# Contrast adjustment on one core: 64 KB rows in three buffers, tiles moved in four transfers of every 4th row, the arithmetic shared by ScalarE and VectorE

## The chip, the cores and the metric

One Trainium2 chip, one of its cores. The metric is the device time of one execution in microseconds (us), median of several runs. The profile's span is about 2 us shorter than the timed run (before: 237.3 against 239.31). Engines: DVE is VectorE, ACT is ScalarE, PE is TensorE, SP issues the loads. "DMA engines" are the core's 16 transfer engines.

## The reference

```python
x: float32 [16, 3, 512, 512]; factor = 1.5
mean = np.mean(x, axis=(2, 3), keepdims=True)
return np.clip(mean + factor * (x - mean), 0, 1).astype(np.float32)
```

Each image plane (1 MB) needs its mean before any of its pixels can be written. 50.33 MB come in and 50.33 MB go out.

## The kernel before

Twelve tiles of 128 rows by 8192 columns (4.2 MB) in a ring of six buffers. DVE and ACT sum each row in two parts; two small matmuls with a block matrix add the rows of an image and give the shift; DVE scales and clips in place.

```python
ROW = 8192; BUFS = 6; SHORT = 2048; SUM = 4352
...
def compute(t):
    xt = ring[:, t % BUFS, :]
    nc.vector.tensor_reduce(out=own[:, 0:1], in_=xt[:, 0:SUM], ...)
    nc.scalar.activation(out=junk, in_=xt[:, SUM:ROW], func=Act.Copy, accum_out=own[:, 1:2])
    # two matmuls: shift = bias[:, t : t + 1] (PSUM)
    for n in FIRST if t == 0 else [ROW]:
        nc.vector.tensor_scalar(out=part, in0=part, scalar1=factor, scalar2=shift, op0=mult, op1=add)
        nc.vector.tensor_scalar(out=part, in0=part, scalar1=0.0, scalar2=1.0, op0=max, op1=min)
        store(t, c, c + n)          # issued by ACT, 128 rows
...
load(0, c1=SHORT); load(0, c0=SHORT); load(1); load(2, n=2); load(4, n=2)   # issued by SP
for t in range(n_tiles):
    compute(t)
    if t + BUFS < n_tiles:
        load(t + BUFS)              # waits until the store of tile t has landed
```

## Time and profile before

| | before |
|---|---|
| time, median of 5 runs beside the changed kernel | 239.30 us |
| span of the profile | 237.3 us |
| DVE / ACT busy | 163.1 / 43.2 us |
| bytes moved, mean rate | 100.66 MB, 424 GB/s |

The DMA row has "9" in all slices but the first and last, and the span is the bytes over the mean rate, 100.66 MB at 424 GB/s = 237.4 us.

### The profile page before, as it was taken

The page shows a single profiled execution, that of the slowest core. Times are in us where ns is not written, and L with a number is a line of the kernel's source. Part 1 is how long each engine was busy: PE and PEld are TensorE (multiplying, and loading weights), DVE is VectorE, ACT ScalarE, POOL GpSimd, SP SyncE. Part 2 cuts the span into 40 slices and gives each one's busy share as a digit, 9 for nine tenths or more (in the row PEclk, how much of TensorE's full clock was granted, in tenths as well). Part 3 has the DMA queues.
Part 4 walks back from the last instruction along what each step waited for, and adds up shares of the span by engine and source line. Part 5 has one row for each costly group of instructions (what it writes and reads, how often), then busy time and mean ns, then how long its engine had stood idle before and what let it go on. Part 6 is the DMA issues. An engine that isn't in the chain of part 4 may idle for free.

```text
span 237.3 us, 285 instructions
## 1 busy us (share of the span) xinstructions
PE 14.1 (6%) x48; PEld 12.0 (5%) x48; DVE 163.1 (69%) x38; ACT 43.2 (18%) x25; POOL 0.9 (0%) x9
## 2 busy tenths in 40 slices
PE   0010010001010001010010100100100100010000
PEld 0010010001010001010010100100100100010000
DVE  0079989048989328999989898891892795687000
ACT  2050230041050023050320504101400500500000
POOL 1000000000000000000000000000000000000000
DMA  7999999999999999999999999999999999999996
GB/s 297 410 442 442 421 442 359 456 439 441 442 436 414 403 431 442 442 442 442 436 442 436 414 409 425 442 442 442 442 436 442 436 420 403 425 442 442 442 442 265
DMA packets 3712, 100.66 MB, mean 424 GB/s; under 512 B 384, under 2 KB 384, under 8 KB 384
## 3 DMA queue, kind: packets, MB, share of 16 engines
q1 hardware_dynamic: 1840, 50.33, 49.7%
q10 hardware_dynamic: 1872, 50.33, 49.2%
HBM read 50.33 MB, written 50.33 MB: 424 GB/s over the span
## 4 chain that ended last, share of the span: by engine, by line
DMA 57%; DVE 29%; another core or an unknown queue 3%; PE 1%; SPq 1%; issue 0%; DVEq 0%
DMA ring<-in_x_dram 41%; DMA out_dram<-ring 16%; DVE sums L81 10%; DVE ring L91 9%; DVE ring L94 9%; PE bias L87 1%; SPq L76 1%; DVEq L91 0%
## 5 line engine op out<-in xcount | busy, mean ns | idle before, releaser
L81 DVE TENSOR_REDUCE sums<-ring 128x1 f32<-128x4352 f32 x12 | 56.2, 4683 | 45.7 <-DMA ring<-in_x_dram 45.7
L84 ACT ACTIVATE junk<-ring 128x3840 f32<-128x3840 f32 x12 | 40.8, 3403 | 163.3 <-DMA ring<-in_x_dram 107.5
L91 DVE TENSOR_SCALAR ring<-ring,bias 128x8192 f32<-128x8192 f32 (+2 forms) x13 | 54.1, 4163 | 8.9 <-PE bias L87 7.4
L94 DVE TENSOR_SCALAR ring<-ring 128x8192 f32<-128x8192 f32 (+2 forms) x13 | 53.3, 4099 | 0.4
L86 PE MATMUL bias<-sums,blockw 128*128 128x1 f32 x24 | 7.0, 361 | 190.8 <-ACT junk L84 190.8
L86 PEld LDWEIGHTS bias<-sums,blockw 128*128 128x128 f32 x24 | 6.0, 312 | 191.7 <-ACT junk L84 175.2
L87 PE MATMUL bias<-sums,blockw 128*128 128x1 f32 x24 | 7.0, 363 | 4.3 <-DVE sums L81 3.9
L87 PEld LDWEIGHTS bias<-sums,blockw 128*128 128x128 f32 x24 | 6.0, 311 | 5.3 <-DVE sums L81 5.0
L84 ACT ACTIVATION_READ_ACCUMULATOR junk<-ring 128x1 f32 x12 | 2.2, 186 | 0.0
L84 ACT ACT_TABLE_LOAD x1 | 1.3, 1283 | 0.7 <-PEq L129 0.7
L63 POOL MEMSET blockw<- 32x32 f32 x4 | 0.5, 117 | 0.2
L61 POOL MEMSET blockw<- 128x128 f32 x1 | 0.2, 204 | 0.3 <-POOLq L129 0.3
L129 POOL MEMSET const-bfloat16-1.0<- 128x1 bf16 x1 | 0.1, 111 | 0.0
L129 POOL MEMSET const-uint8-127<- 128x1 uint8 x1 | 0.1, 111 | 0.0
L129 POOL MEMSET const-float32-1.0<- 128x1 f32 x1 | 0.1, 108 | 0.0
L129 POOL MEMSET const-float32-0.0<- 128x1 f32 x1 | 0.1, 103 | 0.2 <-issue 0.2
## 6 DMA issues: line engine op xcount, KB each, us to landing
out_dram<-ring ACTq DMA_DIRECT2D x11, 4096.0 KB, 35.8
ring<-in_x_dram SPq DMA_DIRECT2D x7, 4096.0 KB, 49.7
ring<-in_x_dram SPq DMA_DIRECT2D x2, 8192.0 KB, 66.7
ring<-in_x_dram SPq DMA_DIRECT2D x1, 3072.0 KB, 11.7
out_dram<-ring ACTq DMA_DIRECT2D x1, 3072.0 KB, 28.2
ring<-in_x_dram SPq DMA_DIRECT2D x1, 1024.0 KB, 4.8
out_dram<-ring ACTq DMA_DIRECT2D x1, 1024.0 KB, 17.5
```

The source lines that it names most:

```text
L61: nc.gpsimd.memset(blockw, 0.0)
L63: nc.gpsimd.memset(blockw[a : a + ppi, a : a + ppi], wconst)
L76: nc.sync.dma_start(out=ring[:, b : b + n, c0:c1], in_=src)
L81: nc.vector.tensor_reduce(out=own[:, 0:1], in_=xt[:, 0:SUM], axis=mybir.AxisListType.X, op=Alu.add)
L84: nc.scalar.activation(out=junk, in_=xt[:, SUM:ROW], func=Act.Copy, accum_out=own[:, 1:2])
L86: nc.tensor.matmul(shift, blockw, own[:, 1:2], start=True, stop=False)
L87: nc.tensor.matmul(shift, blockw, own[:, 0:1], start=False, stop=True)
L91: nc.vector.tensor_scalar(out=part, in0=part, scalar1=factor, scalar2=shift, op0=Alu.mult, op1=Alu.add)
L94: nc.vector.tensor_scalar(out=part, in0=part, scalar1=0.0, scalar2=1.0, op0=Alu.max, op1=Alu.min)
L129: nc = _bacc.Bacc("TRN2", target_bir_lowering=False, num_devices=1)
```

## The change

Its intent: fewer and larger packets (64 KB rows); buffers given back in quarters, so that three double-size buffers do as well as six; a lighter DVE. A quarter is every 4th row of the tile, 32 rows.

```diff
-ROW = 8192
-BUFS = 6
+ROW = 16384
+BUFS = 3
+OWN = 5120
+CHUNKS = (6144, 5120)
+PARTS = 4
...
+        ext = bass.AP(tensor=..., offset=(t * P + q) * ROW + c0,
+            ap=[[parts * ROW, P // parts], [1, c1 - c0]])
+        rows = ring[q::parts, t % BUFS, c0:c1]
...
+        nc.scalar.activation(out=xt[:, SUM:ROW], in_=xt[:, SUM:ROW], func=Act.Copy, accum_out=...)
...                                                  # DVE does its own columns 0:OWN, then
+        for n in CHUNKS:
+            nc.scalar.activation(out=part, in_=part, func=Act.Relu, bias=shift, scale=factor)
+            nc.vector.tensor_scalar(out=part, in0=part, scalar1=1.0, scalar2=None, op0=Alu.min)
...
+            if t == 0: store(t, parts=PARTS, c1=SHORT)      # an early store of 256 KB
...
         load(0, c1=SHORT)
         load(0, c0=SHORT)
         load(1)
-        load(2, n=2)
-        load(4, n=2)
+        load(2)
         for t in range(n_tiles):
             compute(t)
+            if t == n_tiles - 1:                            # last tile: two column pieces, 128 rows each
+                store(t, c1=cut); store(t, c0=cut)
+            elif t + BUFS < n_tiles:
+                for q in range(PARTS): store(t, q, PARTS, ...)
+                for q in range(PARTS): load(t + BUFS, q, PARTS)
+            else:
+                store(t)
```

So the first three loads and the last three stores are whole (128 rows), and the stores of tiles 0 to 2 and the loads of tiles 3 to 5 are quarters (32 rows).

More of the change, by code (lines that the diff above doesn't have):

```diff
@@ L10 @@
 P = 128
-ROW = 8192
-BUFS = 6
+ROW = 16384
+BUFS = 3
 SHORT = 2048
-FIRST = (SHORT, ROW - SHORT)
-SUM = 4352
+OWN = 5120
+CHUNKS = (6144, 5120)
+SUM = 8704
+PARTS = 4
 @with_exitstack
@@ L39 @@
     assert ppi * ROW == n_pix and per_tile * n_tiles == n_img
+    assert OWN + sum(CHUNKS) == ROW
     factor = float(factor)
@@ L45 @@
     out_f = out.rearrange("b c h w -> (b c h w)")
-    def dram(ap, t, c0=0, c1=ROW):
-        return bass.AP(tensor=ap.tensor, offset=t * P * ROW + c0, ap=[[ROW, P], [1, c1 - c0]])
-    consts = ctx.enter_context(tc.tile_pool(name="consts", bufs=1))
     xpool = ctx.enter_context(tc.tile_pool(name="xpool", bufs=1))
@@ L53 @@
     psum = ctx.enter_context(tc.tile_pool(name="psum", bufs=1, space=bass.MemoryType.PSUM))
-    sums = small.tile([P, 2 * n_tiles], f32, name="sums")
-    junk = small.tile([P, ROW - SUM], f32, name="junk")
-    bias = psum.tile([P, n_tiles], f32, name="bias")
-    blockw = consts.tile([P, P], f32, name="blockw")
-    nc.gpsimd.memset(blockw, 0.0)
-    for a in range(0, P, ppi):
-        nc.gpsimd.memset(blockw[a : a + ppi, a : a + ppi], wconst)
-    ring = xpool.tile([P, BUFS, ROW], f32, name="ring")
@@ L68, in load @@
-    def load(t, c0=0, c1=ROW, n=1):
-        b = t % BUFS
-        src = bass.AP(
-            tensor=x_f.tensor,
-            offset=t * P * ROW + c0,
-            ap=[[ROW, P], [P * ROW, n], [1, c1 - c0]],
-        )
-        nc.sync.dma_start(out=ring[:, b : b + n, c0:c1], in_=src)
+    ring = xpool.tile([P, BUFS, ROW], f32, name="ring")
+    sums = small.tile([P, n_tiles, 2], f32, name="sums")
+    bias = small.tile([P, n_tiles], f32, name="bias")
+    pbias = psum.tile([P, n_tiles], f32, name="pbias")
@@ new lines, with move @@
+    blockw = small.tile([P, P], f32, name="blockw")
+    nc.gpsimd.memset(blockw, 0.0)
+    for a in range(0, P, 2 * ppi):
+        mid, end = a + ppi, a + 2 * ppi
+        nc.gpsimd.memset(blockw[a:end, mid:end], wconst)
+        nc.gpsimd.memset(blockw[a:mid, mid:end], 0.0)
+        nc.gpsimd.memset(blockw[a:mid, a:mid], wconst)
+    def move(engine, to, source, t, q, parts, c0, c1):
+        ext = bass.AP(
+            tensor=(source if to is ring else to).tensor,
+            offset=(t * P + q) * ROW + c0,
+            ap=[[parts * ROW, P // parts], [1, c1 - c0]],
+        )
+        rows = ring[q::parts, t % BUFS, c0:c1]
+        if to is ring:
+            engine.dma_start(out=rows, in_=ext)
+        else:
+            engine.dma_start(out=ext, in_=rows)
@@ L78, in compute, with load, store @@
+    def load(t, q=0, parts=1, c0=0, c1=ROW):
+        move(nc.sync, ring, x_f, t, q, parts, c0, c1)
+    def store(t, q=0, parts=1, c0=0, c1=ROW):
+        move(nc.scalar, out_f, ring, t, q, parts, c0, c1)
     def compute(t):
         xt = ring[:, t % BUFS, :]
-        own = sums[:, 2 * t : 2 * t + 2]
         nc.vector.tensor_reduce(
-            out=own[:, 0:1], in_=xt[:, 0:SUM], axis=mybir.AxisListType.X, op=Alu.add
+            out=sums[:, t, 0:1], in_=xt[:, 0:SUM], axis=mybir.AxisListType.X, op=Alu.add
@@ L83, in compute @@
         )
-        nc.scalar.activation(out=junk, in_=xt[:, SUM:ROW], func=Act.Copy, accum_out=own[:, 1:2])
-        shift = bias[:, t : t + 1]
-        nc.tensor.matmul(shift, blockw, own[:, 1:2], start=True, stop=False)
-        nc.tensor.matmul(shift, blockw, own[:, 0:1], start=False, stop=True)
-        c = 0
-        for n in FIRST if t == 0 else [ROW]:
-            part = xt[:, c : c + n]
-            nc.vector.tensor_scalar(
-                out=part, in0=part, scalar1=factor, scalar2=shift, op0=Alu.mult, op1=Alu.add
-            )
-            nc.vector.tensor_scalar(
-                out=part, in0=part, scalar1=0.0, scalar2=1.0, op0=Alu.max, op1=Alu.min
-            )
-            store(t, c, c + n)
+        nc.scalar.activation(
+            out=xt[:, SUM:ROW],
+            in_=xt[:, SUM:ROW],
+            func=Act.Copy,
+            accum_out=sums[:, t, 1:2],
+        )
@@ new lines, in compute @@
+        for j in (1, 0):
+            nc.tensor.matmul(
+                pbias[:, t : t + 1], blockw, sums[:, t, j : j + 1], start=j == 1, stop=j == 0
+            )
+        shift = bias[:, t : t + 1]
+        nc.vector.tensor_copy(out=shift, in_=pbias[:, t : t + 1])
+        own = xt[:, 0:OWN]
+        nc.vector.tensor_scalar(
+            out=own, in0=own, scalar1=factor, scalar2=shift, op0=Alu.mult, op1=Alu.add
+        )
+        nc.vector.tensor_scalar(
+            out=own, in0=own, scalar1=0.0, scalar2=1.0, op0=Alu.max, op1=Alu.min
+        )
@@ L98, in compute @@
+        c = OWN
+        for n in CHUNKS:
+            part = xt[:, c : c + n]
+            nc.scalar.activation(out=part, in_=part, func=Act.Relu, bias=shift, scale=factor)
+            nc.vector.tensor_scalar(out=part, in0=part, scalar1=1.0, scalar2=None, op0=Alu.min)
             c += n
-    def store(t, c0, c1):
-        nc.scalar.dma_start(out=dram(out_f, t, c0, c1), in_=ring[:, t % BUFS, c0:c1])
+            if c == ROW:
+                break
+            if t == 0:
+                store(t, parts=PARTS, c1=SHORT)
@@ L106 @@
         load(1)
-        load(2, n=2)
-        load(4, n=2)
+        load(2)
         for t in range(n_tiles):
             compute(t)
-            if t + BUFS < n_tiles:
-                load(t + BUFS)
+            if t == n_tiles - 1:
+                cut = ROW - CHUNKS[-1]
+                store(t, c1=cut)
+                store(t, c0=cut)
+            elif t + BUFS < n_tiles:
+                for q in range(PARTS):
+                    store(t, q, PARTS, c0=SHORT if t + q == 0 else 0)
+                for q in range(PARTS):
+                    load(t + BUFS, q, PARTS)
+            else:
+                store(t)
 _INS = ['x', 'factor']
```

## The prediction

> **What bounds the kernel now.** I read the page's engine table and its 40 slices first. In the slices below, the first line is DVE's busy tenths, the second the DMA engines', the third the GB/s they moved; the two queue lines give packets, bytes and the share of all 16 engines' span.
>
> ```profile
> span 237.3 us, 285 instructions
> ...
> DVE  0079989048989328999989898891892795687000
> ...
> DMA  7999999999999999999999999999999999999996
> GB/s 297 410 442 442 421 442 359 456 439 441 442 436 414 403 431 442 442 442 442 436 442 436 414 409 425 442 442 442 442 436 442 436 420 403 425 442 442 442 442 265
> ...
> q1 hardware_dynamic: 1840, 50.33, 49.7%
> q10 hardware_dynamic: 1872, 50.33, 49.2%
> ```
>
> The DMA engines are at "9" in every slice but the first and last, and the two queues (q1 loads, q10 stores) fill 98.9% of the span between them. DVE (69%) has empty slices, ACT (18%) hardly works. The kernel is one uninterrupted transfer of 100.66 MB.
>
> Next the table by stages (stretch in us, its length, each engine's busy time, clock, DMA share, GB/s): loads and stores mixed, then the end, when only stores are left.
>
> ```profile
> 21.00:60.00 39.00, 2.35 (x8) 2.00 (x8) 28.66 (x7) 6.99 (x4) 0.00 (x0) 1.00 0.99 417
> 60.00:203.70 143.70, 9.39 (x32) 8.02 (x32) 113.49 (x26) 27.97 (x16) 0.00 (x0) 1.00 1.01 434
> 203.70:236.00 32.30, 1.18 (x4) 1.01 (x4) 13.60 (x3) 3.50 (x2) 0.00 (x0) 1.00 0.98 422
> ```
>
> The rate is the same whoever computes, so computing hides beside the transfers. That holds in the tail too: the last tile comes in at 203.8 and its store is issued at 218.2 us, while the store queue is still draining.
>
> ```profile
> 203.76 4.69 DVE L81 TENSOR_REDUCE sums<-ring 128x1 f32<-128x4352 f32 x1 [4.98 <-DMA ring<-in_x_dram]
> ...
> 218.17 0.34 ACTq L101 DMA_DIRECT2D out_dram<-ring  x1
> ```
>
> Last the waits of the load queue (waits in total us, times, longest): loads wait 139 us for stores to free a buffer, and it costs nothing, because the engines then work on those very stores.
>
> ```profile
> SPq L76 <- DMA out_dram<-ring: 138.9, 7, 25.5
> ```
>
> The chain of waits gives DVE 29%, but I don't take that as a bound: it steps through tiles whose computing ran under full DMA engines.
>
> **The floor in packets.** The trace's DMA packet records give the usual duration of one row's packet: 309 ns for 8 KB, 912 for 24 KB, 1213 for 32 KB. The last step is 301 ns per 8 KB (27.2 GB/s an engine) and about 8 ns are left over as fixed cost. One engine carries 8 rows of each 128-row transfer: per direction 8 x 309 + 8 x 912 + 88 x 1213 = 116.5 us, 233.0 for both. (Check: 116.5 / 237.3 = 49.1%, and the page has 49.2% for q10.) The first packet starts at 1.7 us, the last ends at 236.0: 234.3 us, thus 1.3 us idle in all. About 1.3 us follow.
>
> [...]
>
> **The change, part by part.**
> *Rows of 64 KB.* Half as many packets. A 64 KB packet should take 8 x 301 + 8 = 2417 ns, against 2 x 1213 = 2426. In the new count (8 x 309 + 8 x 2118 + 40 x 2417 = 116.1 us per direction, the stores the same within 0.1) this makes 232.2 us against 233.0: **0.8 us gained**, on the path.
> *Computing per tile (8.4 MB, 6 of them).* DVE: reduce of 8704, at most 2 x 4683 = 9.3 us; copy of the shift 0.2 (my guess); from the 8192- and 6144-column rows (4491 and 3418; 4427 and 3359 ns) 5120 columns take 2.88 + 2.83; the two min passes 3.36 and 2.83. Sum 21.4, times 6 = 128 us against 163. [...] From tile landed to last store: 9.3 + 0.6 (matmuls) + 0.2 + 5.4 + 4.55 + 2.83 = **22.9 us** (before: 14.4). A tile's turn of DMA time is 38.7 us (16 packets of 2.417), so neither engine becomes the bound.
> *Three buffers.* The ring holds the same 192 KB per partition, but a buffer is now twice as much, so turns matter. My ledger, per engine, with equal turns when both queues have work (a load and a store packet 4.83 us):
> Load 0 done 21.1, landed 22.6 (landing lags 1.4 us in the trace: packets end at 11.5, reduce starts at 12.96). Stores of tile 0 issued 46 (20.9 before), first packets near 50 (the first store lagged 3.7 us behind its issue). Until then loads run alone: 19.7 of the 24 ring rows. Load 2 ends 71. Store 0 frees its quarters at 60, 70, 80, 90; load 3 uses them from 71 on: **queue never dry**, ends 109. Store 1 runs 88 to 126, load 4 109 to 148; store 2 126 to 165, load 5 148 to 187. Each quarter is free about 10 us before its load is due. Tiles 1 to 4 are ready at about 69, 95, 134, 173, before their store turns of 88, 126, 165, 195. Tail: load 5 landed 188.4; sums, shift, own part, first chunk and the second Relu are done at 208.5, when its first store is issued. Stores 3 and 4 keep the engines busy to 214.6. So **about 5 us slack**, and no bubble.
> *Quarters instead of whole tiles* free buffers earlier, and add DMA issues of some 0.34 us on queues with time to spare. *In-place sum, scratch gone*: frees memory, no time.
> Sum: 237.3 - 0.8 = 236.5 us span; the timed run was 239.31, 2.0 above, hence 238.5. I allow 0.3 for small gaps: **238.8 us**.
>
> **Rivals.** *Quarter transfers run slower.* [...] The three quartered loads and stores are 50 MB, 116 us; a rate 10% lower there costs 13 us (116 / 0.9 - 116) and makes 252. For: no such transfer is in the trace. [...] *The tail opens.* If stores get more than half of the turns, loads end later and the 5 us slack goes: each us by which load 5 lands later, after that, is one us more; 241 to 244. Against: when the last load of before landed at 203.8, some 32 us of stores were left, so stores did not get ahead of loads; and their late start (46 us) helps. *A buffer comes free late* (coarse tiles, completion lag): 10 us slack per quarter speaks against; one miss costs 1 to 3 us. *A gain over 2%* needs under 234.5 us, below the 232.2 us of packets plus 1.7 + 1.3 + 2.0 = 237.2[...]. *DVE's relief shortens it*: no, its 35 us lie beside the transfers.
>
> **Range and chances.** The mechanism leaves 237.2 to about 240; the tail and quarters reach up. Range 236.8 to 245. Faster 0.03; slower 0.15, nearly all from slow quarters; within 2% 0.82.
>
> **What would show it.** Packets of 64 KB, about half as many; mean GB/s in the mixed stretch 434 or a little over; DVE near 128 us, ACT near 100; DMA slices at 9 throughout. A slice under 9 near 205 to 217 would be the tail rival; [...] long waits of the load queue with empty DMA slices, the buffer rival. What would make me wrong is foremost how 32 spread rows are dealt to 16 engines.

ACT's sum came to 16.8 us a tile (6.6 for the sum of 7680 columns, 0.2 for the read of the accumulator, 5.4 and 4.55 for the two Relu passes) and 100 us for six. In the changed kernel's trace they are 6.60, 0.19, 5.42 and 4.55, 16.8 in all. The 5.4 and 4.55 are also in the 22.9 us from landing to last store; in proportion to the 3403 ns that 3840 columns take in the trace before, they are estimated at 5.4 and 4.5. The "equal turns" of the ledger are in that trace, too: 944 load packets and 960 store packets start between 60 and 203.7 us. Slow quarter transfers: this rival is the author's estimate alone; its sign: under 420 GB/s between 60 and 165 us with full slices.

## The result, and the profile after

The changed kernel takes 244.65 us (244.24 to 244.81, five runs) against 239.30 us: ratio 1.0221, 95% interval 1.0207 to 1.0235, so slower by more than 2%. A ratio here is the mean time of one kernel's fast runs over that of the other's of the same rounds, so it is not quite the ratio of the medians.

The page of the changed kernel, the same rows as before:

```profile
span 242.4 us, 244 instructions
...
DVE  0002988897847700198940078989810068980000
...
DMA  8999999999999999999999999999999899989984
GB/s 324 454 454 422 422 443 422 389 346 476 346 422 443 433 433 433 433 433 433 433 433 433 433 433 433 433 433 433 433 433 378 346 465 400 476 389 427 454 383 176
...
q1 hardware_dynamic: 1152, 50.33, 49.6%
q10 hardware_dynamic: 1200, 50.33, 48.2%
```

The packets fell from 3712 to 2353. From slice 13 to slice 29 the rate is a steady 433. But there are low slices near slice 8 to 10, low ones at 30 and 31 (counted from 0), and a ragged end. The table by stages (stretch, length, busy time of each engine, clock, DMA share, GB/s) puts numbers on them:

```profile
48.00:75.00 27.00, 1.01 (x4) 0.93 (x4) 20.20 (x7) 16.57 (x4) 0.00 (x0) 1.00 1.00 388
75.00:180.00 105.00, 3.20 (x12) 2.85 (x12) 62.62 (x18) 49.70 (x12) 0.00 (x0) 1.00 1.00 434
180.00:192.00 12.00, 0.00 (x0) 0.00 (x0) 0.00 (x0) 0.00 (x0) 0.00 (x0) 1.00 0.96 371
192.00:218.00 26.00, 1.18 (x4) 1.00 (x4) 20.55 (x6) 16.57 (x4) 0.00 (x0) 1.00 0.99 431
```

The important point is the first line: DMA share 1.00, yet only 388 GB/s. The engines don't stand still, their packets take longer (3.0 to 4.0 us near 62 us in place of 2.4). The same at 180 to 192 (0.96, 371 GB/s). (These views count a packet whole in the stretch where it starts. One round of 16 packets of 64 KB is 1.05 MB, which is 39 GB/s over 27 us and 87 over 12, so a rate in a short stretch is only a pointer; the durations of the packets below decide.) The whole of the long middle runs at 434, and so does the stretch where only stores are left, up to 218.

The last microseconds of the changed kernel, in the same form:

```profile
236.00:239.00 3.00, 0.00 (x0) 0.00 (x0) 0.00 (x0) 0.00 (x0) 0.00 (x0) 1.00 0.78 335
239.00:242.40 3.40, 0.00 (x0) 0.00 (x0) 0.00 (x0) 0.00 (x0) 0.00 (x0) 1.00 0.14 60
```

and of the kernel before:

```profile
232.00:235.00 3.00, 0.00 (x0) 0.00 (x0) 0.00 (x0) 0.00 (x0) 0.00 (x0) 1.00 0.99 426
235.00:237.30 2.30, 0.00 (x0) 0.00 (x0) 0.00 (x0) 0.00 (x0) 0.00 (x0) 1.00 0.00 0
```

Before, all 16 engines finish nearly together: their 16 completion records of the last store lie between 235.8 and 236.4 us. After, some are done 3 us ahead of others (238.1 to 241.5 us), and those idle. (Slice 35 of the page, from 212 us, shows an "8", which the prediction had named as a sign of its tail rival. The packet records show all 16 engines busy there; the digit comes from where packets start.)

The trace's packet records allow a full account, in us per DMA engine, from the first packet to the last. "Usual" prices every row at the usual duration of its size (309 ns for 8 KB, 1213 for 32 KB, 2418 for 64 KB); "longer" is what the packets took beyond that; "idle" is the rest.

| | usual | longer | idle | first to last packet |
|---|---|---|---|---|
| before | 233.0 | 1.3 | 0.0 | 234.3 |
| after | 232.3 | 4.6 | 2.5 | 239.4 |

The difference, -0.7 + 3.3 + 2.5 = 5.1 us, is the difference of the spans. Of the 4.6 us longer, 2.8 lie between 36 and 72 us, 1.2 between 174 and 198 and 0.5 at the start (before, the start has 0.7). 4.0 of the 4.6 us are on load packets. Of the 2.5 us idle, about 0.5 lie near 187 us and 2.0 at the end.

### The profile page after: what moved, and what is told of

Read it like the earlier page. It is cut to its first block, busy times and chain, and to the rows that moved or that the text cites. A ratio compares the mean times of both kernels' runs of the same rounds, so it can differ in the third digit from the quotient of the medians.

```text
span 242.4 us, 244 instructions
## 1 busy us (share of the span) xinstructions
PE 6.5 (3%) x24; PEld 5.8 (2%) x24; DVE 126.8 (52%) x36; ACT 100.8 (42%) x25; POOL 1.4 (1%) x17
## 4 chain that ended last, share of the span: by engine, by line
DMA 69%; DVE 12%; ACT 6%; ACTq 1%; PE 0%; issue 0%; SPq 0%; DVEq 0%
DMA out_dram<-ring 51%; DMA ring<-in_x_dram 19%; DVE sums L92 8%; ACT ring L119 6%; DVE ring L120 2%; DVE ring L110 1%; DVE ring L113 1%; ACTq L82 1%; PE pbias L104 0%; SPq L80 0%; DVE bias L108 0%; DVEq L92 0%; ACTq L119 0%
## 5 line engine op out<-in xcount | busy, mean ns | idle before, releaser
L96 ACT ACTIVATE ring<-ring 128x7680 f32<-128x7680 f32 x6 | 39.6, 6602 | 99.5 <-DMA out_dram<-ring 48.4
L92 DVE TENSOR_REDUCE sums<-ring 128x1 f32<-128x8704 f32 x6 | 55.3, 9216 | 46.1 <-DMA ring<-in_x_dram 46.1
L119 ACT ACTIVATE ring<-ring,bias 128x6144 f32<-128x6144 f32 (+1 forms) x12 | 59.3, 4984 | 14.8 <-DVE bias L108 13.9
L120 DVE TENSOR_SCALAR ring<-ring 128x6144 f32<-128x6144 f32 (+1 forms) x12 | 37.1, 3091 | 6.7 <-ACT ring L119 6.7
L108 DVE COPY bias<-pbias 128x1 f32<-128x1 f32 x6 | 0.9, 158 | 38.5 <-PE pbias L104 38.5
L110 DVE TENSOR_SCALAR ring<-ring,bias 128x5120 f32<-128x5120 f32 x6 | 17.3, 2886 | 0.2
L113 DVE TENSOR_SCALAR ring<-ring 128x5120 f32<-128x5120 f32 x6 | 17.0, 2827 | 0.2
L104 PE MATMUL pbias<-sums,blockw 128*128 128x1 f32 x24 | 6.5, 358 | 199.1 <-ACT ring L96 193.9
L104 PEld LDWEIGHTS pbias<-sums,blockw 128*128 128x128 f32 x24 | 5.8, 316 | 199.7 <-ACT ring L96 165.1
L96 ACT ACTIVATION_READ_ACCUMULATOR ring<-ring 128x1 f32 x6 | 1.1, 186 | 0.0
```

Source lines behind the costliest of these rows:

```text
L92: nc.vector.tensor_reduce(out=sums[:, t, 0:1], in_=xt[:, 0:SUM], axis=mybir.AxisListType.X, op=Alu.add)
L96: nc.scalar.activation(out=xt[:, SUM:ROW], in_=xt[:, SUM:ROW], func=Act.Copy, accum_out=sums[:, t, 1:2],)
L104: nc.tensor.matmul(pbias[:, t : t + 1], blockw, sums[:, t, j : j + 1], start=j == 1, stop=j == 0)
L108: nc.vector.tensor_copy(out=shift, in_=pbias[:, t : t + 1])
L110: nc.vector.tensor_scalar(out=own, in0=own, scalar1=factor, scalar2=shift, op0=Alu.mult, op1=Alu.add)
L113: nc.vector.tensor_scalar(out=own, in0=own, scalar1=0.0, scalar2=1.0, op0=Alu.max, op1=Alu.min)
```

## The experiments

**Theory M (mix).** Both slow stretches are places where a transfer of 128 rows in one direction meets quarters of 32 rows in the other: at 48 to 75 us the whole load of tile 2 and the quarter stores of tile 0; at 180 to 192 us the quarter loads of tile 5 and the whole store of tile 3. In the long middle both directions are quarters. Rivals: the quarters or the 64 KB rows themselves cost when stores begin (Q, R, S), the load queue runs out (L), or the HBM side does it (H).

### e1: quarters everywhere that loads and stores meet

```diff
-        load(0, c1=SHORT); load(0, c0=SHORT); load(1); load(2)
+        for t in range(BUFS):
+            for q in range(PARTS):
+                load(t, q, PARTS)
...
+            elif t == n_tiles - BUFS:
+                for q in range(PARTS):
+                    store(t, q, PARTS)
```

> The changed kernel, but the first three loads and the store of tile 3 are also cut into four transfers of every 4th row, so that no load of 128 rows is in flight beside a store of 32 rows or the reverse. Theory M (mixing 128-row and 32-row transfers slows packets): the slices near 48 to 70 and 180 to 195 us, 346 to 422 GB/s in the changed kernel, come back to 433; span 242.4 - 3.3 (longer packets) - 2 (engines ending at different times) = about 237, timed 238.5 to 239.5. Rival Q (quarter transfers, or 64 KB rows, cost by themselves when stores begin and end): stays at 243 to 246, as there are more of them.

Measured: 253.26 us, ratio 1.0588, against both theories. The edit had a side effect. Twelve loads don't go out at once. In the trace all transfers, of both queues, share eight completion semaphores (the changed kernel's 33 issues name eight, too), and here the issues wait for one that is still in use: six loads went out at once, the seventh waited until 13.3 us for the second to land, the eighth until 23.0 for the fourth, and the ninth until 43.4 for the early small store. The waits for earlier loads alone are 25.3 us, as the first of these lines says (waited for, us in total, times, longest). So the load queue ran dry near 45 us, the loads fell behind, and the engines stood still ahead of the last store:

```profile
SPq L80 <- DMA ring<-in_x_dram: 25.3, 3, 9.2
```

```profile
42.00:48.00 6.00, 0.00 (x0) 0.00 (x0) 4.04 (x3) 2.12 (x1) 0.00 (x0) 1.00 0.80 304
...
75.00:204.00 129.00, 3.52 (x12) 3.01 (x12) 63.56 (x18) 49.70 (x12) 0.00 (x0) 1.00 1.01 436
...
222.00:228.00 6.00, 0.00 (x0) 0.00 (x0) 5.97 (x3) 6.00 (x2) 0.00 (x0) 1.00 0.00 0
```

The 180 to 192 us stretch lies inside the 436 of the middle line, which speaks for M there; on the first stretch the rate decides nothing, as the queue ran dry. But at 50 us a round of load packets took 3.3 to 4.0 us in place of 2.4 although loads and stores were quarters, which M doesn't explain. It shows, too, that the tail has little slack: the last load landed at 209.1 us, and DVE and ACT work for 19.1 us before the last tile's first store is issued at 228.2.

### e2: quarters by columns, all with 128 rows

```diff
-                    store(t, q, PARTS, c0=SHORT if t + q == 0 else 0)
+                    store(t, c0=SHORT if t + q == 0 else q * n, c1=(q + 1) * n)
-                    load(t + BUFS, q, PARTS)
+                    load(t + BUFS, c0=q * n, c1=(q + 1) * n)
```

(The early small store is whole in this run, too.)

> The changed kernel with the quarters cut by columns: each transfer has all 128 rows, 16 KB of each. As many transfers and the same release of buffers by quarters, but only one row shape. Theory M: no slow stretch where the first stores meet the first loads (over 425 GB/s there), timed 239 to 241, the packets' fixed 8 ns costing under 1 us. Rival Q (cutting in four costs) or rival S (the stretch is slow because stores begin beside old loads, whatever their shape): slow stretches stay, 243 to 246.

Measured: 257.06 us, ratio 1.0734, a miss for both. The rate at 48 to 75 us rose from 388 to 404. The time was lost in the tail:

```profile
216.00:234.00 18.00, 1.01 (x4) 0.93 (x4) 8.85 (x4) 15.38 (x4) 0.00 (x0) 1.00 0.02 7
```

The last load's quarters have 16 KB rows and meet a whole store with 64 KB rows. In the trace of the kernel before, such queues take turns packet by packet: between 24.6 and 36.6 us the first store's 128 packets of 8 KB start beside 119 load packets of 32 KB. With such turns the load here would get a fifth of the bytes as long as both have work (an estimate from the row lengths); it landed only at 217.3 us.

### e3: the opposite, more mixing

```diff
+                if t == 0:
                     for q in range(PARTS):
                         store(t, q, PARTS, c0=SHORT if t + q == 0 else 0)
+                else:
+                    store(t)
```

> The changed kernel with the stores of tiles 1 and 2 whole (128 rows), the loads of tiles 3 to 5 still in quarters of every 4th row. Theory M: where both queues work between 75 and 190 us, the rate falls from 433 to 360 to 400 GB/s with all DMA engines busy; total over 248. Rivals Q and S: rate stays 433 while both work; only gaps from buffers that come free late, total 243 to 247.

Measured: 248.76 us in the one run (state unknown). M's sign is right, and the total; but the loss is not spread over all the time in which both queues work. It comes in stretches of some 12 us with full rate between them:

```profile
102.00:114.00 12.00, 0.00 (x0) 0.00 (x0) 0.00 (x0) 0.00 (x0) 0.00 (x0) 1.00 0.97 371
114.00:138.00 24.00, 1.17 (x4) 1.00 (x4) 18.36 (x5) 16.43 (x4) 0.00 (x0) 1.00 1.01 437
138.00:150.00 12.00, 0.00 (x0) 0.00 (x0) 2.83 (x1) 0.13 (x1) 0.00 (x0) 1.00 0.97 377
150.00:168.00 18.00, 0.00 (x0) 0.00 (x0) 0.00 (x0) 0.00 (x0) 0.00 (x0) 1.00 1.02 437
```

From 112 to 129 us only stores run, so the second line says nothing about mixing. The fourth does: quarter loads and a whole store run there together, and nearly all packets take the usual 2418 ns. So M has to be put more narrowly: mixing costs at certain moments, for a few rounds of packets, after which the engines run freely again, still mixed.

### e4: the HBM side

```diff
-            offset=(t * P + q) * ROW + c0,
-            ap=[[parts * ROW, P // parts], [1, c1 - c0]],
+            offset=(t * P + q * (P // parts)) * ROW + c0,
+            ap=[[ROW, P // parts], [1, c1 - c0]],
```

> Wrong result on purpose: the quarters still take every 4th row of the on-chip buffer but 32 consecutive rows in HBM. Theory M on the on-chip side: the slow stretches near 48 to 70 and 180 to 195 us stay, time 244 to 246. Rival H (the HBM side, rows 256 KB apart beside consecutive ones): they vanish, 238 to 240.

Measured: 244.79 us in one run, result wrong as meant; 386 GB/s at 48 to 75 us, 437 in the middle, 360 at 180 to 192. Its packet records lose 2.9 us from 36 to 72 and 1.0 from 174 to 198, against 2.8 and 1.2. As M expected, nothing came back. The pattern of addresses in HBM is not the cause.

### x1, x2, x3: one meeting at a time

x1 cuts only the store of tile 3 (the second diff part of e1). x2 cuts only the load of tile 2:

```diff
-        load(2)
+        for q in range(PARTS):
+            load(2, q, PARTS)
```

x3 does both. With seven loads at the start, e1's side effect is not quite gone in x2, against its expectation: five went out at once, the sixth at 22.3 us and the seventh at 47.9, when the early small store had landed (the load queue waited 19.0 us for an earlier load). It did not stop the engines: they idle 0.0 us from 40 to 60.

> The changed kernel with one more store cut: tile 3 leaves in quarters of every 4th row too, so that the loads of tile 5 (quarters) no longer meet a whole-tile store. Theory M (a change of row shape while both queues work costs): the stretch 180 to 192 us comes back from 371 to about 433 GB/s (1.7 us) and the engines end closer together; timed 241 to 243. Rival L (that stretch is slow because the load queue runs out there): it stays slow, 244 to 246. The first slow stretch (48 to 75 us, 388 GB/s) stays in both.

> The changed kernel with only the load of tile 2 cut into quarters of every 4th row: it is the load beside which the first quarter stores run. All seven loads are still issued at once. Theory M: 48 to 75 us comes back from 388 to over 420 GB/s, timed 241.5 to 243. Rival S (the first stores slow the loads because all 16 DMA engines start them in step, whatever the shape): it stays near 388, 244 to 246.

> The two edits together: load of tile 2 and store of tile 3 both in quarters. Theory M: both slow stretches gone, 239 to 241. Rival S and L: 244 to 246 or more, since load 5 lands no earlier and the tail has little slack.

| | time | ratio to before | 48 to 75 us | 75 to 180 us | 180 to 192 us |
|---|---|---|---|---|---|
| changed kernel | 244.65 | 1.0221 | 388 GB/s | 434 | 371 |
| x1: store 3 cut | 241.78 | 1.0099 | 379 | 438 | 437 |
| x2: load 2 cut | 245.57 | 1.0256 | 418 | 426 | 388 |
| x3: both | 242.87 | 1.0152 | 418 | 428 | 431 |

The rates form a square: each edit mends its own stretch and hardly touches the other. The lines of x1, then of x2, for the two slow stretches:

```profile
48.00:75.00 27.00, 1.01 (x4) 0.93 (x4) 19.51 (x7) 16.57 (x4) 0.00 (x0) 1.00 0.98 379
...
180.00:192.00 12.00, 0.00 (x0) 0.00 (x0) 4.08 (x3) 2.27 (x2) 0.00 (x0) 1.00 1.01 437
```

```profile
48.00:75.00 27.00, 1.01 (x4) 0.93 (x4) 19.43 (x6) 16.57 (x4) 0.00 (x0) 1.00 1.01 418
...
180.00:192.00 12.00, 0.00 (x0) 0.00 (x0) 0.00 (x0) 0.00 (x0) 0.00 (x0) 1.00 0.93 388
```

The packet records show the square more sharply. "Longer", by when a packet starts, and "idle", in us per engine:

| | longer, 36 to 54 us | 54 to 72 us | 72 to 174 us | 174 to 198 us | idle, in all |
|---|---|---|---|---|---|
| before | 0.5 | 0.0 | 0.0 | 0.0 | 0.0 |
| changed kernel | 1.2 | 1.6 | 0.1 | 1.2 | 2.5 |
| x1: store 3 cut | 1.4 | 1.7 | 0.0 | 0.0 | 1.4 |
| x2: load 2 cut | 1.4 | 0.2 | 0.9 | 1.3 | 3.7 |
| x3: both | 1.5 | 0.2 | 0.8 | 0.1 | 2.6 |

M holds from 54 to 72 and from 174 to 198 us. L falls, as the second stretch is mended in x1 although its load queue runs out there, too. S stands for what is left, 36 to 54 us: there it is mostly one round of load packets just before the first full store, 3.2 to 3.9 us each in x2 and x3, whatever the rows. Each kernel has such a round: x4 below, with whole transfers only, at 60 us (3.2 to 3.7 us), and the kernel before at 38 us (1.5 to 1.8 in place of 1.2 us).

In time the second mix is worth 244.65 - 241.78 = 2.9 us, and x1 lies inside M's forecast of 241 to 243: 1.2 us of longer packets, the 0.5 us of idle time near 187 us, and part of the uneven finish.

Mending the first stretch brought no time, and x2 and x3 miss M's forecasts. In x2 the packets from 54 to 72 us give 1.4 us, but those from 72 to 174 take back 0.8, and the idle time grows by 1.2: the last load landed at 201.4 us in place of 195.8, and a gap of about 2 us opened ahead of the last store. In that middle, in x2 and x3, an engine moves two rows of loads, then two of stores, and about a fifth of the load packets are longer (up to 3.5 us in x2). Why they are, stays open. So does the uneven finish: x3 mixes at neither place, and 2.6 us of idle time remain at its end.

### x4: whole transfers only

```diff
-PARTS = 4
+PARTS = 1
```

> The changed kernel with whole transfers of 128 rows only (four parts set to one): rows of 64 KB, three buffers and the split of the computing stay. Theory M: no slow stretch where stores first meet loads (over 425 GB/s), but a buffer comes free only when its whole store has landed, so load 5 lands some 10 us later and the engines run dry ahead of the last store: 243 to 250. Rival R (64 KB rows are what slows the first stores): the slow stretch stays as well, 388 GB/s.

Measured: 244.56 us (242.64 to 245.26), ratio 1.0206, 95% interval 1.0161 to 1.0250, so whether it is more than 2% slower is unclear. 425 GB/s at 48 to 75 us. So R falls but for the one round of loads before the first full store, which is here as well. The last load landed at 201.8 us and the expected gap opened:

```profile
48.00:75.00 27.00, 1.18 (x4) 1.01 (x4) 25.31 (x7) 20.77 (x5) 0.00 (x0) 1.00 1.03 425
...
216.00:222.00 6.00, 0.00 (x0) 0.00 (x0) 5.06 (x3) 5.77 (x2) 0.00 (x0) 1.00 0.28 120
```

The quarters thus do buy what they were made for, an earlier last load (195.8 us in place of 201.8), and pay about as much for it.

### x5: x4 with the last tile in two column pieces

```diff
+                    if t + BUFS == n_tiles - 1:
+                        load(t + BUFS, c1=SUM)
+                        load(t + BUFS, c0=SUM)
...          # last tile: ACT sums SUM:12800, DVE the rest; columns 0:OWN are stored first
```

> The whole-transfer kernel (x4: 128 rows only, rows of 64 KB, three buffers, a gap of some 5 us between 216 and 222 us) with the last tile loaded in two column pieces, its last sum shared by both engines and its own part stored first. If the gap comes from the 19 us between the last landing and the first store of that tile, it closes: shift ready some 5 us sooner, first store issued another 3 us sooner, timed 244.56 - 5.3 = 238.9 to 239.8. If the gap has another cause (the engines slow after the loads), it stays near 244.

Measured: 257.66 us, ratio 1.0768, a clear miss. The computing did what was hoped: from landing to the first store 10.9 us in place of 19.1. But the landing itself moved from 201.8 to 223.3 us. The likely reason is that of e2: rows of 34 and 30 KB run beside store rows of 64 KB, and with turns packet by packet the load gets about a third of the bytes (an estimate from the row lengths). The engines also slowed: the last of these lines has 386 GB/s at a full DMA share, and the 64 KB store packets there mostly take 2.7 to 3.2 us in place of 2.4. All transfers have 128 rows, so a mix of 128-row and 32-row transfers is not the only thing that makes packets longer.

```profile
223.29 3.89 DVE L108 TENSOR_REDUCE extra<-ring 128x1 f32<-128x3584 f32 x1 [19.20 <-DMA ring<-in_x_dram]
...
234.14 0.34 ACTq L84 DMA_DIRECT2D out_dram<-ring  x1
```

```profile
192.00:216.00 24.00, 0.59 (x2) 0.50 (x2) 9.22 (x1) 0.00 (x0) 0.00 (x0) 1.00 1.02 386
```

### y1: the computing alone, on the transfers of before

ROW and BUFS as before; OWN = 2560, chunks of 3072 and 2560, the sum in place.

> The kernel before with the change's computing alone (sum in place, ScalarE does scale, shift and Relu on about two thirds of a row, VectorE the rest and the minimum), its transfers and six buffers untouched. Theory: computing lies beside the transfers, 239.0 to 239.7. Rival C (ScalarE issues the stores and is now busy, so stores start later): 240 to 243.

Measured: 239.56 us, ratio 1.0018 (1.0004 to 1.0032). DVE falls to 132.3 us busy, ACT rises to 105.4, and the time rises by 0.4 us (0.1 to 0.8). On these transfers the computing part of the change is nearly neutral.

### y2: x1 without the early small store

> x1 (store of tile 3 in quarters) without the early 256 KB store of tile 0. The slow load packets at 49 us follow directly on the end of that small store. If ending a first store while loads run is what costs there, one of the slow rounds goes: 48 to 75 us from 379 to 395 or more, timed 240.5 to 241.2. If the row shapes alone cost, the stretch stays at 375 to 390 and the time at 241.5 to 242.2.

Measured: 241.94 us, 388 GB/s at 48 to 75 us, as expected if the early store costs nothing: it is not the cause.

### y3: 32 neighbouring rows

```diff
-        rows = ring[q::parts, t % BUFS, c0:c1]
+        n = P // parts
+        rows = ring[q * n : q * n + n, t % BUFS, c0:c1]
```

(with the HBM side of e4, so the result is right again)

> The changed kernel with quarters of 32 neighbouring rows instead of every 4th. If what counts is which part of the on-chip memory the rows lie in [...], 75 to 180 us falls from 434 to 220 to 350 GB/s and the total passes 280. If only the number of rows counts, it stays at 434 and 243 to 246.

Measured: 293.63 us in one run. The middle, where both directions are quarters:

```profile
75.00:180.00 105.00, 2.02 (x8) 1.85 (x8) 39.42 (x11) 32.09 (x8) 0.00 (x0) 1.00 0.98 310
```

310 GB/s at a DMA share of 0.98: all the engines are at work, slower. Against e4 (437 GB/s there, with the same HBM addresses) only the rows of the on-chip memory that a transfer names are different.

**What is shown and what is argued.** The packets account for 5.8 us lost (3.3 longer, 2.5 idle). Shown: some 3 us of them (1.4 from 54 to 72 us, 1.2 and 0.5 of idle time near 187) come from whole and quarter transfers meeting, as they go when the transfers are cut alike (x1, x2, x3), and not from HBM addresses (e4: 386 and 360 GB/s in the two stretches), the early store (y2: 388 in the first) or the computing (y1: 0.4 us). Shown, too, that the place of the rows on chip can set the rate (y3: 310 GB/s in place of 437). Not shown: what makes the round before the first full store slow (36 to 54 us have 1.2 us, against 0.5 before), and what makes the finish uneven (2.0 us).

How a meeting slows packets is not shown: no view names the engine of a packet. The packet records of the changed kernel show load packets of 3.3 to 3.7 us at 49 us and 3.0 to 4.0 at 62, in rounds that all 16 engines start within 0.4 us and 0.7 us. From 65 us on the packets are back at 2418 ns, while the whole load of tile 2 still meets quarter stores until 74; all that has changed to the eye is that the engines form two groups of eight, 0.7 us apart. So the order in which the engines fall may matter as much as the sets of rows; that is argued only. x2 and x3 changed both, and no run changed that order alone.

## Why the prediction was right or wrong

The measured 244.65 lies inside the range, near its upper end of 245.0. The central value, 238.8, was 5.9 us low, and "slower" had been given only 0.15. That the range held, by 0.35 us, is partly luck: its upper part was made for slow quarters and an opening tail, and the loss came from neither.

- *What bounds the kernel*: right. y1 took 31 us of work off DVE and changed the time by 0.4 us.
- *The floor in packets*: right. A 64 KB packet usually takes 2418 ns (2417 expected), and the usual sum is 232.3 us (232.2). The gain of 0.7 us is there, and small.
- *Computing per tile*: right. DVE 126.8 us (128), ACT 100.8 (100), and tile 4 takes 176.7 - 153.8 = 22.9 us from its reduce to its store, as worked out.
- *The ledger of the buffers*: nearly right. The loads never ran dry in a way that cost time, but the last one landed at 195.8 us, not 188.4. It left out that ACT, which issues the stores, had to wait at the second quarter of a store until an earlier transfer had given back its semaphore (that of tile 1 was issued at 74.4 us, as tile 0's second quarter, with the same semaphore, had landed at 74.38):

```profile
ACT ring L96 <- DMA out_dram<-ring: 48.4, 2, 27.5
```

  so tile 2 was stored from 115 us on, not from 95. Its turn came only when the store of tile 1 was done, near 132 us (126 in the ledger), so the delay was hidden. What made the last load 7.4 us late is not fully accounted for; the 2.8 us of longer packets between 36 and 72 us are part of it.
- *The tail, 5 us of slack and no bubble*: right in effect (431 GB/s from 192 to 218, and the packet records have no idle time there), with less slack than stated. The first of these lines is the landing, the second the first store of the last tile, issued at 214.9 in place of 208.5:

```profile
195.75 9.22 DVE L92 TENSOR_REDUCE sums<-ring 128x1 f32<-128x8704 f32 x1 [19.08 <-DMA ring<-in_x_dram]
...
214.90 4.11 ACTq L82 DMA_DIRECT2D out_dram<-ring  x2
```

- *The step that failed* is the allowance: "1.3 us idle in all. About 1.3 us follow", and 0.3 us for small gaps. The 1.3 us before were not idle time but packets longer than usual, at the start and around the first stores. After the change that term is 4.6 us, and 2.5 us of true idle time come on top: 7.1 us in place of 1.6.
- *The rival "Quarter transfers run slower"* looked at the wrong place, and its reason is shown by no run: quarters among themselves run at 434 GB/s, so the 13 us over 116 us did not come. The part of the loss that is explained, some 3 us, is in the few rounds where quarters meet whole tiles. The prediction read the quarter transfers alone and never asked which transfers of the other direction they would meet.

No version with the changed transfers beat the kernel before. The best, x1, stays 1% behind.

## What to carry to other kernels

When the DMA engines are busy in every slice, read the rate beside the busy share: a share of 1.00 at 388 GB/s is a loss that no idle time shows. In a short stretch, check it on the packets' durations. Cut the transfers of both directions alike wherever they will be in flight together, in their set of rows (here the packets else took 1.4 and 1.2 us longer per engine in the two stretches) and in row length (with shorter rows the last load landed at 223.3 us in place of 201.8, x5 against x4). It is no cure-all: x3 does so in their sets of rows, has 1.7 us less of longer packets than the changed kernel, and still stays 1.5% behind the kernel before. And a gain of 0.7 us from larger rows has to be weighed against what the larger tile does to the start and the end.
